# Latent attention heads: row maxima, scores and splits in another order and on another engine

## The chip, the cores and the metric

The kernel runs on one core of a Trainium2 chip. The metric is the device time of one launch in microseconds. Engines: TensorE (PE; its weight loads are shown apart, as PEld), VectorE (DVE), ScalarE (ACT), GpSimd (POOL), and SyncE (SP), whose queue issues most DMAs.

## The reference

Two transformer layers on 1024 positions of width 1024, float32. The change touches the mixer of the first, latent attention with 12 causal heads of width 96 (64 without and 32 with rotary position):

```
q = (rmsnorm(c_q) @ w_uq).reshape(b, s, 12, 96)        # rope on the last 32
k = concat([k_nope, rope(k_r) for every head])
sc = einsum('bqhd,bkhd->bhqk', q, k) * 96 ** -0.5
p = softmax(where(k_idx <= t_idx, sc, -1e30))
o = einsum('bhqk,bkhd->bqhd', p, v)                    # v: 64 wide
```

Memory cross-attention, an output projection, a second mixer and two large MLPs follow; they take most of the time and are untouched.

## The kernel before

**Precision.** A float32 operand x is split in two (helper `split`, L96): hi is a copy made by ScalarE (L99) in the type that TensorE reads fast, lo = x - hi, the rest, by VectorE (L100). A product is then three: hi hi, hi lo, lo hi.

**Head operands.** `head_tiles(h)` (L868) loads a head's queries and keys by four DMAs into q32 and k32 (96x1024, one buffer each; in the trace q and k) and splits them into qh, ql, kh, kl. Three sets of these are used in turn; the set of heads 1, 4, 7, 10 lies in older tiles and is called ckh and ckl in the trace. It is called two heads ahead, at the first block of head h - 2.

**Row maxima.** Softmax needs each query row's maximum before the scores. `row_max(h, i)` (L897) makes row tile i (128 queries): a product of the high parts over (i+1)*128 keys into a tile psx (L908), and a VectorE instruction that adds the causal mask `wide` and reduces to a column m (L915). For i > 3 psx is one tile of two banks with one buffer; lower rows use the common one-bank tiles, of which there are six. `max_row(h)` (L886) transposes the eight columns (psxt, L889), copies them (mh, L894) and writes them by a DMA (L895) into row 96 of qh, so that the score product subtracts the maximum by itself.

**Blocks.** A head has 12 score blocks (G, k): keys of tile k against query half G. Blocks with k >= 4G lie on the diagonal; their first 128 columns are masked, and at diagonal offset c = k - 4G they are 512 - 128c wide. Their order is the list `blocks` (L1006). `scores` (L1032) makes three products into a tile pss (L1023), and a fourth for the mask where `mask_by_pe` says so; else VectorE adds it (L1045). ScalarE takes the exponential into p (L1047, 12 buffers). GpSimd adds the p of a head up in acc (L1060).

**Order.** All products of this loop go on TensorE in the order in which the code issues them (L1178 ff.): block n of all heads; then the row maxima that the table `WHEN` sets there, as pairs (row, distance in blocks from the start of the head before; row 8 is `max_row`); every six blocks `values` (p times v, tile pso); after block 7 the `sums` of the head before (acc times ones, psd). `evac` and the stores of the denominators go through SP's queue. Heads 0 to 5, 6 to 9 and 10 are divided by their sums in later blocks (`rc_split`, `rc_mul`: loads of tiles rb, multiplies on VectorE). From block 116 on, weights of the output projection are split too (woq).

Of the kernel before, what the change touches and what calls it, by code (L numbers as in the profile page):

```python
# [55 lines left out]
def trunk(  # L56
# [25 lines left out]
    def ps1(name):  # L82
        return psum[0].tile([P, 512], F32, tag="m", bufs=4 if len(psum) == 1 else 6, name=name)
# [12 lines left out]
    def split(src, hi, lo, scale=None):  # L96

        if scale is None:
            a = nc.scalar.activation(hi, src, AF.Copy)  # L99
            d = nc.vector.tensor_tensor(lo, src, f32(hi), ALU.subtract)  # L100
        else:
            a = nc.scalar.activation(hi, src, AF.Copy, scale=scale)
            d = nc.vector.scalar_tensor_tensor(lo, src, scale, f32(hi), ALU.mult, ALU.subtract)
        return a.ins, d.ins
# [765 lines left out]
    def head_tiles(h):  # L870
        r = slice((h % 2) * 64, (h % 2) * 64 + 64)
        q32 = hb.tile([96, S], F32, tag="q32", bufs=1, name=f"q32_{h}")
        k32 = hb.tile([96, S], F32, tag="k32", bufs=1, name=f"k32_{h}")
        nc.sync.dma_start(out=q32[0:64], in_=qn[h // 2][r, :])
        nc.sync.dma_start(out=q32[64:96], in_=qr[h // 4][(h % 4) * 32 : (h % 4) * 32 + 32, :])
        nc.sync.dma_start(out=k32[0:64], in_=kn[h // 2][r, :])
        nc.sync.dma_start(out=k32[64:96], in_=krs)
        qh, ql, kh, kl = bufs_[h % 3]
        if h in (1, 2):
            head_ones(h)  # L880
        split(q32, qh[0:96], ql[0:96])
        split(k32, kh[0:96], kl[0:96])

    m8s, wide = {}, []

# [12 lines left out]
    def row_max(h, i):  # L898
        if h not in m8s:
            m8s[h] = hb.tile([P, NT], F32, tag="m8", bufs=2, name=f"m8_{h}")  # L900
        qh, ql, kh, kl = bufs_[h % 3]
        n = (i + 1) * P
        ps = psx(f"psx{h}_{i}") if i > 3 else ps1(f"psx{h}_{i}")
        cuts = [(0, 320), (320, 640)] if n == 640 else [(a, min(a + 512, n)) for a in range(0, n, 512)]
        if n == 640:
            ps = ps[:, 192:]
        for a, b in cuts:
            mm = nc.tensor.matmul(ps[:, a:b], qh[0:96, i * P : (i + 1) * P], kh[0:96, a:b], start=True, stop=True, skip_group_check=True)  # L908
        m = m8s[h][:, i : i + 1]
        least = 3.0e38  # L910
        if h == 0 and i:
            nc.vector.reduce_max(m, ps[:, : n - P], axis=AX, negate=True)
            least = m
        o, k = (ps[:, n - P : n], dmask) if h == 0 else (ps[:, :n], wide[0][:, S - n :])
        nc.vector.tensor_tensor_reduce(o, o, k, -1.0, least, ALU.add, ALU.min, accum_out=m)  # L915
        return mm.ins
# [86 lines left out]
    nc.gpsimd.tensor_copy(identr, ident)  # L1003
    nc.gpsimd.tensor_copy(maskr, dmaskT)

    blocks = [(1, 0), (0, 0), (1, 4), (0, 1), (1, 5), (1, 1), (0, 2), (1, 6), (1, 2), (0, 3), (1, 7), (1, 3)]  # L1006
    blocks_end = [(1, k) for k in (0, 4, 5, 6, 7, 1, 2, 3)] + [(0, k) for k in range(4)]

    def mask_by_pe(h, G, k):
        return k >= 4 * G and (k % 2 == 1 or h in (0, 1, 7, 9, 10, 11))  # L1010


    def blocks_of(h):
# [15 lines left out]

        return [(part ^ G, max(c0, part * 256), part * 256 + 256) for part in range(2) if c0 < part * 256 + 256]  # L1030

    def scores(h, G, k):  # L1032

        qh, ql, kh, kl = bufs_[h % 3]
        c0 = col0(G, k)
        ks = slice(k * P, (k + 1) * P)
        qs = slice(G * 512 + c0, G * 512 + 512)
        ps = ps1(f"pss{h}_{G}_{k}")[:, c0:]
        product(ps, kh[:, ks], qh[:, qs], start=True, stop=False)
        product(ps, kh[:, ks], ql[:, qs], start=False, stop=False)  # L1040
        if mask_by_pe(h, G, k):
            product(ps[:, 0:P], identr, maskr, start=False, stop=False)
        product(ps, kl[:, ks], qh[:, qs], start=False, stop=True)
        if k >= 4 * G and not mask_by_pe(h, G, k):
            nc.vector.tensor_tensor(ps[:, 0:P], ps[:, 0:P], dmaskT, ALU.add)  # L1045
        p = at.tile([P, 512], F32, tag="p", bufs=12, name=f"p{h}_{G}_{k}")
        masked[0:1] = [nc.scalar.activation(p[:, c0:], ps, AF.Exp, scale=SC).ins]  # L1047
        probs[(h, G, k)] = p
        if (h, "acc") not in acc_:
            acc_[(h, "acc")] = at.tile([P, 1024], F32, tag="acc", bufs=2, name=f"acc{h}")  # L1050
        a = acc_[(h, "acc")][:, G * 512 : G * 512 + 512]
        if (h, G) not in first_p:
            first_p[(h, G)] = p
            return
        q = first_p[(h, G)]
        if q is not None:
            first_p[(h, G)] = None
            if c0:
                nc.scalar.activation(a[:, :c0], q[:, :c0], AF.Copy)
        nc.gpsimd.tensor_tensor(a[:, c0:], p[:, c0:], (a if q is None else q)[:, c0:], ALU.add)  # L1060
# [85 lines left out]
    def rc_mul(c):  # L1146
# [17 lines left out]
    seq = [(h,) + b for h in range(H) for b in blocks_of(h)]  # L1164

    WHEN = {
# [3 lines left out]
    }  # L1170
    ahead = {}
    for h in range(1, H):
        for i, d in WHEN[min(h, 3)]:
            ahead.setdefault((h - 1) * NB + d, []).append((h, i))
    muls = iter(())
    cuts = [*range(0, (H - 1) * NB, 6), *range((H - 1) * NB, len(seq) + 1, 4)]
    batches = {b + 1: (a, b) for a, b in zip(cuts, cuts[1:])}
    for n in range(len(seq) + 2):  # L1178
        if n < len(seq):
            scores(*seq[n])  # L1180
        for g, i in ahead.get(n, ()):
            with queued():
                last_mm[0:1] = [row_max(g, i) if i < NT else max_row(g)[-1]]
        if n in batches:
            values(seq[slice(*batches[n])])
            h, j = divmod(n, NB)
            if j == 1 and h < H:
                evac(h - 1)
            if h and j == (7 if h < H - 1 else 5):
                sums(h - 1)  # L1190
            if n == len(seq) - 3:
                sums(H - 1, 1)
                last_o(1, at.tile([P, 256], F32, tag="on", bufs=2, name="rq1"))
        h, j = divmod(n, NB)
        if n < len(seq):
            if h and j == 0 and h + 2 < H:
                head_tiles(h + 2)
            if n == 5:
                with tc.issue_after(masked[0]):
                    head_tiles(2)  # L1200
        if n % 2 or n > 11 * NB:
            next(muls, None)
        if n >= 9 * NB + 8 and n % 3 == 0:
            wq.step()
        for c in range(3):
            if n == GRP[c + 1] * NB + (8 if c == 2 else 10):
                rc_split(c)
            if n == GRP[c + 1] * NB + (9 if c == 2 else 13):
                muls = rc_mul(c)
# [1115 lines left out]
```

## Time and profile before

| | us |
|---|---|
| median of 3 runs | 2089.3 (2088.59 to 2093.86) |
| profiled execution | 2089.84 |
| its span | 2088.1 |
| TensorE busy in it | 2060.1 |
| VectorE busy in it | 1433.5 |
| ScalarE busy in it | 1090.2 |
| GpSimd busy in it | 258.3 |

The span is the time from the first to the last instruction; 1.7 us of the execution lie outside it. All times of single instructions are counted from the span's start. The heads of the latent attention run from about 239 to 432 us. In a row of the order of time, a bracket at the end is the idle time of that engine just before, and what ended it; `x3` means three instructions shown together.

### The profile page before, as it was taken

What the parts mean: (1) busy time and instruction counts of PE and PEld (TensorE: products, weight loads), DVE (VectorE), ACT (ScalarE), POOL (GpSimd) and SP (SyncE); (2) the same over time, 40 slices, a digit from 0 to 9 for tenths busy, and PEclk for the clock granted to TensorE, in tenths of its full rate; (3) what the DMA queues carried; (4) which work ended last, traced back from release to release, by engine and by line L of the source; (5) the groups of instructions that cost most, each with busy time, mean ns of one, the idle gap of its engine ahead of it and who ended that gap; (6) DMA issues with size and microseconds to landing.
All of it is one profiled execution on the core that took longest, in us unless ns stands there. A gap on an engine that the chain in (4) does not pass through costs nothing.

```text
span 2088.1 us, 29578 instructions
## 1 busy us (share of the span) xinstructions
PE 2060.1 (99%) x10067; PEld 1684.8 (81%) x10067; DVE 1433.5 (69%) x2829; ACT 1090.2 (52%) x2359; POOL 258.3 (12%) x363
## 2 busy tenths in 40 slices
PE   9999999999999999999999999999999999999998
PEld 6988777678888888888888888778888888888887
DVE  8766566665977777976557535666977776976565
ACT  7554355566745544444445435766755544444453
POOL 1001256621000000000011133420000000000000
PEclk9999899999999999999999999999999999999999
DMA  6302223352444546944443544542344546945442
GB/s 225 104 1 77 57 69 76 112 162 86 147 153 141 166 161 234 331 124 153 142 118 104 147 106 125 139 135 78 136 150 158 166 146 227 331 139 156 121 121 87
DMA packets 183496, 292.88 MB, mean 140 GB/s; under 512 B 17707, under 2 KB 73456, under 8 KB 183344
## 3 DMA queue, kind: packets, MB, share of 16 engines
q1 hardware_dynamic: 177680, 275.17, 42.2%
q0 software_dynamic: 4144, 13.14, 1.7%
q10 hardware_dynamic: 1520, 2.68, 0.4%
q8 instruction: 79, 1.29, 0.3%
q14 instruction: 73, 0.60, 0.1%
HBM read 187.60 MB, written 81.44 MB: 129 GB/s over the span
## 4 chain that ended last, share of the span: by engine, by line
PE 94%; DVE 2%; ACT 1%; DMA 1%; issue 1%; SPq 0%; ACTq 0%; DVEq 0%
PE psy L1899 6%; PE psy L1897 6%; PE psy L1898 6%; PE psu L1560 6%; PE psu L1561 5%; PE psu L1559 5%; PE psz L1899 4%; PE psz L1897 4%; PE psz L1898 4%; PE psv L1560 4%; PE psv L1561 4%; PE psv L1559 4%; PE pss L1023 4%; PE pswo L111 3%; PE pswo L109 3%; PE pswo L110 3%
## 5 line engine op out<-in xcount | busy, mean ns | idle before, releaser
L99 ACT ACTIVATE g<-i 128x512 fp32r<-128x512 f32 x79 | 49.9, 631 | 104.1 <-PE psy L1898 53.3
L1897 PE MATMUL psy<-g 128*128 128x512 f32 x256 | 100.0, 391 | 0.0
L1898 PE MATMUL psy<-g 128*128 128x512 f32 x256 | 99.7, 389 | 0.0
L1899 PE MATMUL psy<-g 128*128 128x512 f32 x256 | 99.7, 389 | 0.0
L1060 POOL TENSOR_TENSOR acc<-p,acc 128x384 f32<-128x384 f32 (+3 forms) x96 | 93.7, 994 | 31.9 <-ACT p L1047 30.5
L915 DVE CUSTOM_DVE_ANT_0 psx<-psx,wide 128x1024 f32<-128x1024 f32 (+5 forms) x88 | 66.4, 765 | 43.8 <-PE psx L908 42.8
L100 DVE TENSOR_TENSOR g<-i,g 128x512 fp32r<-128x512 f32 x79 | 55.7, 705 | 51.7 <-ACT g L99 51.7
L1047 ACT ACTIVATE p<-pss 128x512 f32<-128x512 f32 (+3 forms) x144 | 67.2, 487 | 41.8 <-PE pss L1023 30.6
L99 ACT ACTIVATE uh<-i 128x512 fp32r<-128x512 f32 x66 | 41.6, 631 | 85.2 <-PE psz L1898 39.2
L99 ACT ACTIVATE i<-mr 128x512 fp32r<-128x512 f32 x78 | 47.9, 630 | 72.7 <-PE psy L1898 23.7
L100 DVE TENSOR_TENSOR uh<-i,uh 128x512 fp32r<-128x512 f32 x66 | 45.6, 691 | 46.5 <-ACT uh L99 46.5
L1899 PE MATMUL psz<-g 128*128 128x512 f32 x192 | 74.7, 389 | 0.0
L1897 PE MATMUL psz<-g 128*128 128x512 f32 x192 | 74.7, 389 | 0.0
L1898 PE MATMUL psz<-g 128*128 128x512 f32 x192 | 74.7, 389 | 0.0
L1458 ACT ACTIVATE mr<-mr,gcol 128x256 f32<-128x256 f32 (+1 forms) x160 | 64.0, 477 | 11.6 <-DMA mr<-in_mlp_w_up_dram 11.6
L100 DVE TENSOR_TENSOR i<-mr,i 128x512 fp32r<-128x512 f32 x78 | 53.7, 688 | 21.6 <-ACT i L99 21.6
L2017 POOL TENSOR_TENSOR wsr<-wsr,gcol 128x1024 f32<-128x1024 f32 x12 | 23.0, 1918 | 345.8 <-ACT i L99 276.7
L1779 DVE TENSOR_TENSOR mqq<-mqf,mqq 128x512 f32<-128x512 f32 x64 | 43.2, 688 | 22.7 <-DMA mqf<-in_mlp_w_down_dram 22.6
L1899 PEld LDWEIGHTS psy<-g 128*128 128x128 f32 x256 | 48.1, 188 | 10.0
L1897 PEld LDWEIGHTS psy<-g 128*128 128x128 f32 x256 | 48.1, 188 | 9.8
L1898 PEld LDWEIGHTS psy<-g 128*128 128x128 f32 x256 | 48.1, 188 | 9.8
L1023 PE MATMUL pso<-p,v 128*64 128x256 f32 (+1 forms) x480 | 54.6, 371 | 0.0
(670 smaller groups left out, 6825.6 us busy)
## 6 DMA issues: line engine op xcount, KB each, us to landing
i<-hd SPq DMA_DIRECT2D x154, 256.0 KB
hd<-uh SPq DMA_DIRECT2D x76, 256.0 KB
hd<-ul SPq DMA_DIRECT2D x76, 256.0 KB
mr<-in_mlp_w_up_dram SPq DMA_DIRECT2D x36, 512.0 KB
hd<-x SPq DMA_DIRECT2D x72, 256.0 KB
mr<-hd SPq DMA_DIRECT2D x70, 256.0 KB
d<-in_mlp_w_up_dram SPq DMA_DIRECT2D x32, 512.0 KB
mqf<-in_mlp_w_down_dram SPq DMA_DIRECT2D x32, 512.0 KB
```

What stands on the lines that cost most here:

```text
L99: a = nc.scalar.activation(hi, src, AF.Copy)
L100: d = nc.vector.tensor_tensor(lo, src, f32(hi), ALU.subtract)
L915: nc.vector.tensor_tensor_reduce(o, o, k, -1.0, least, ALU.add, ALU.min, accum_out=m)
L1023: last_mm[0:1] = [nc.tensor.matmul(*args, skip_group_check=True, **kw).ins]
L1047: masked[0:1] = [nc.scalar.activation(p[:, c0:], ps, AF.Exp, scale=SC).ins]
L1060: nc.gpsimd.tensor_tensor(a[:, c0:], p[:, c0:], (a if q is None else q)[:, c0:], ALU.add)
L1559: nc.tensor.matmul(ps, wh[:, k, :], xh[:, k, :], start=p in (1, 2, 5) and k == 0, stop=False, skip_group_check=True)
L1560: nc.tensor.matmul(ps, wh[:, k, :], xl[:, k, :], start=False, stop=False, skip_group_check=True)
L1561: nc.tensor.matmul(ps, wl[:, k, :], xh[:, k, :], start=False, stop=k == 3, skip_group_check=True)
L1897: nc.tensor.matmul(ps, ah[:, j, :], bh, start=start, stop=False, skip_group_check=True)
L1898: nc.tensor.matmul(ps, ah[:, j, :], bl, start=False, stop=False, skip_group_check=True)
L1899: nc.tensor.matmul(ps, al[:, j, :], bh, start=False, stop=k == NP - 1, skip_group_check=True)
```

## The change

1. `head_tiles`: for heads 2 to 11 the rests ql and kl are made by GpSimd instead of VectorE. The high parts stay on ScalarE.
2. Blocks (0,3) and (1,2) change places in `blocks`.
3. `mask_by_pe`: TensorE masks the diagonal offsets 0 and 1, before 1 and 3, in heads 2 to 6 and 8. Heads 0, 1, 7, 9, 10, 11 still mask all on TensorE.
4. `scores` takes one or two blocks. A block of offset 3 (128 columns) waits for the next one if that is not on the diagonal. For two blocks the first two products of each are issued, the wide block first, then the last product of each.
5. `WHEN`: the rows of all heads come earlier and in other distances.
6. `row_max` of head 0 takes its two-bank tile for all rows.

```
-        split(q32, qh[0:96], ql[0:96])
-        split(k32, kh[0:96], kl[0:96])
+        for src, hi, lo in ((q32, qh, ql), (k32, kh, kl)):
+            if h < 2:
+                split(src, hi[0:96], lo[0:96])
+            else:
+                nc.scalar.activation(hi[0:96], src, AF.Copy)
+                nc.gpsimd.tensor_tensor(lo[0:96], src, f32(hi[0:96]), ALU.subtract)
...
-        ps = psx(f"psx{h}_{i}") if i > 3 else ps1(f"psx{h}_{i}")
+        ps = psx(f"psx{h}_{i}") if i > 3 or len(psum) == 1 else ps1(f"psx{h}_{i}")
...
-    blocks = [(1, 0), (0, 0), (1, 4), (0, 1), (1, 5), (1, 1), (0, 2), (1, 6), (1, 2), (0, 3), (1, 7), (1, 3)]
+    blocks = [(1, 0), (0, 0), (1, 4), (0, 1), (1, 5), (1, 1), (0, 2), (1, 6), (0, 3), (1, 2), (1, 7), (1, 3)]
...
-        return k >= 4 * G and (k % 2 == 1 or h in (0, 1, 7, 9, 10, 11))
+        return k >= 4 * G and (k % 4 < 2 or h in (0, 1, 7, 9, 10, 11))
...
-    def scores(h, G, k):
-
-        qh, ql, kh, kl = bufs_[h % 3]
+    def scores(*todo):
+
+        tiles = []
+        for h, G, k in todo:
+            qh, ql, kh, kl = bufs_[h % 3]
+            c0 = col0(G, k)
+            ks = slice(k * P, (k + 1) * P)
+            qs = slice(G * 512 + c0, G * 512 + 512)
+            ps = ps1(f"pss{h}_{G}_{k}")[:, c0:]
+            product(ps, kh[:, ks], qh[:, qs], start=True, stop=False)
+            product(ps, kh[:, ks], ql[:, qs], start=False, stop=False)
+            tiles.append((ps, kl[:, ks], qh[:, qs]))
+        for (h, G, k), (ps, kl_, qh_) in zip(todo, tiles):
+            if mask_by_pe(h, G, k):
+                product(ps[:, 0:P], identr, maskr, start=False, stop=False)
+            product(ps, kl_, qh_, start=False, stop=True)
+        for block, tile in zip(todo, tiles):
+            probabilities(*block, tile[0])
...
-        3: ((7, -5), (6, -4), (5, -2), (4, 0), (3, 1), (2, 2), (1, 3), (0, 4), (8, 6)),
+        3: ((7, -7), (6, -5), (5, -4), (4, -2), (3, 0), (2, 1), (1, 2), (0, 3), (8, 5)),
...
     for n in range(len(seq) + 2):
         if n < len(seq):
-            scores(*seq[n])
+            waiting.append(seq[n])
+            if n == len(seq) - 1 or seq[n][2] - 4 * seq[n][1] < 3 or seq[n + 1][2] - 4 * seq[n + 1][1] >= 0:
+                scores(*waiting[::-1])
+                waiting.clear()
```

`probabilities` is the rest of the old `scores`: VectorE's mask, the exponential, GpSimd's add. The rows of WHEN for sets 1 and 2 become `((7, 0), (3, 0), (6, 2), (2, 2), (5, 4), (1, 4), (4, 5), (0, 6), (8, 8))` and `((7, -4), (6, -3), (5, -2), (4, 0), (3, 1), (2, 2), (1, 3), (0, 4), (8, 6))`; before, they were `((7, 2), (3, 3), (6, 4), (2, 5), (5, 6), (1, 7), (4, 8), (0, 9), (8, 10))` and `((7, -2), (6, -1), (5, 0), (4, 1), (3, 2), (2, 3), (1, 4), (0, 5), (8, 6))`.

In the rows of the order below pss3_1_7 is the score tile of head 3, G = 1, k = 7, and psx5_6 is row 6 of head 5's maxima; qh0, kh2 and so on are the operands of a head; the number at the end of a name only counts tiles.

TensorE in head 3 before, from row 6 of the maxima of head 5 to row 5:

```order
L908 MATMUL psx5_6_3201<-kh2_2529,qh2_2527 128x512
L908 MATMUL psx5_6_3201<-kh2_2529,qh2_2527 128x384
L1023 MATMUL pss3_0_3_3205<-qh0_1949,kh0_1951 128x128
L1023 MATMUL pss3_0_3_3205<-ql0_1950,kh0_1951 128x128
L1023 MATMUL pss3_0_3_3205<-maskr_2538,identr_2537 128x128
L1023 MATMUL pss3_0_3_3205<-qh0_1949,kl0_1952 128x128
L1023 MATMUL pss3_1_7_3213<-qh0_1949,kh0_1951 128x128
L1023 MATMUL pss3_1_7_3213<-ql0_1950,kh0_1951 128x128
L1023 MATMUL pss3_1_7_3213<-maskr_2538,identr_2537 128x128
L1023 MATMUL pss3_1_7_3213<-qh0_1949,kl0_1952 128x128
L908 MATMUL psx5_5_3221<-kh2_2529,qh2_2527 128x512
L908 MATMUL psx5_5_3221<-kh2_2529,qh2_2527 128x256
```

After, TensorE in the same head from row 7 to row 6:

```order
L912 MATMUL psx5_7_3150<-kh2_2529,qh2_2527 128x512 x2
L1027 MATMUL pss3_0_2_3154<-qh0_1949,kh0_1951 128x256
L1027 MATMUL pss3_0_2_3154<-ql0_1950,kh0_1951 128x256
L1027 MATMUL pss3_0_2_3154<-qh0_1949,kl0_1952 128x256
L1027 MATMUL pss3_1_6_3162<-qh0_1949,kh0_1951 128x256
L1027 MATMUL pss3_1_6_3162<-ql0_1950,kh0_1951 128x256
L1027 MATMUL pss3_1_6_3162<-qh0_1949,kl0_1952 128x256
L912 MATMUL psx5_6_3170<-kh2_2529,qh2_2527 128x512
L912 MATMUL psx5_6_3170<-kh2_2529,qh2_2527 128x384
```

Then values and sums, and after them, still on TensorE, from row 5 to row 4 with the first pair between them:

```order
L912 MATMUL psx5_5_3198<-kh2_2529,qh2_2527 128x512
L912 MATMUL psx5_5_3198<-kh2_2529,qh2_2527 128x256
L1027 MATMUL pss3_1_2_3202<-qh0_1949,kh0_1951 128x512
L1027 MATMUL pss3_1_2_3202<-ql0_1950,kh0_1951 128x512
L1027 MATMUL pss3_0_3_3205<-qh0_1949,kh0_1951 128x128
L1027 MATMUL pss3_0_3_3205<-ql0_1950,kh0_1951 128x128
L1027 MATMUL pss3_1_2_3202<-qh0_1949,kl0_1952 128x512
L1027 MATMUL pss3_0_3_3205<-qh0_1949,kl0_1952 128x128
L912 MATMUL psx5_4_3217<-kh2_2529,qh2_2527 128x320 x2
```

The narrow blocks and their masks no longer stand between rows 6 and 5; rows 7 and 6 have two blocks of 256 columns between them, rows 5 and 4 one pair.

TensorE at the turn from head 0 to head 1 before, rows 7, 6 and 5 of set 2:

```order
L908 MATMUL psx2_7_2697<-kh2_2529,qh2_2527 128x512 x2
L1023 MATMUL pss0_1_3_2701<-qh0_1949,kh0_1951 128x512
L1023 MATMUL pss0_1_3_2701<-ql0_1950,kh0_1951 128x512
L1023 MATMUL pss0_1_3_2701<-qh0_1949,kl0_1952 128x512
L908 MATMUL psx2_6_2708<-kh2_2529,qh2_2527 128x512
L908 MATMUL psx2_6_2708<-kh2_2529,qh2_2527 128x384
L1023 MATMUL pss1_1_0_2712<-ckh_554,ckl_555 128x512 x3
L908 MATMUL psx2_5_2719<-kh2_2529,qh2_2527 128x512
```

and after:

```order
L912 MATMUL psx2_7_2674<-kh2_2529,qh2_2527 128x512 x2
L1027 MATMUL pss0_1_2_2678<-qh0_1949,kh0_1951 128x512
L1027 MATMUL pss0_1_2_2678<-ql0_1950,kh0_1951 128x512
L1027 MATMUL pss0_0_3_2681<-qh0_1949,kh0_1951 128x128
L1027 MATMUL pss0_0_3_2681<-ql0_1950,kh0_1951 128x128
L1027 MATMUL pss0_1_2_2678<-qh0_1949,kl0_1952 128x512
L1027 MATMUL pss0_0_3_2681<-maskr_2538,identr_2537 128x128
L1027 MATMUL pss0_0_3_2681<-qh0_1949,kl0_1952 128x128
L912 MATMUL psx2_6_2693<-kh2_2529,qh2_2527 128x512
L912 MATMUL psx2_6_2693<-kh2_2529,qh2_2527 128x384
L912 MATMUL psx2_5_2697<-kh2_2529,qh2_2527 128x512
L912 MATMUL psx2_5_2697<-kh2_2529,qh2_2527 128x256
```

Row 5 now follows row 6 directly.

GpSimd at the end of head 3 before, the last adds of that head and the first of the next:

```order
L1060 TENSOR_TENSOR acc3_3066<-p3_1_2_3198,acc3_3066 128x512
L1060 TENSOR_TENSOR acc3_3066<-p3_0_3_3210,acc3_3066 128x128
L1060 TENSOR_TENSOR acc3_3066<-p3_1_7_3218,acc3_3066 128x128
L1060 TENSOR_TENSOR acc3_3066<-p3_1_3_3229,acc3_3066 128x512
L1060 TENSOR_TENSOR acc4_3238<-p4_1_4_3280,p4_1_0_3236 128x512
```

and after:

```order
L1074 TENSOR_TENSOR acc3_3070<-p3_1_2_3210,acc3_3070 128x512
L1074 TENSOR_TENSOR acc3_3070<-p3_0_3_3214,acc3_3070 128x128
L886 TENSOR_TENSOR kl0_1952<-k32_6_3247,kh0_1951 96x1024
L1074 TENSOR_TENSOR acc3_3070<-p3_1_3_3229,acc3_3070 128x512
L1074 TENSOR_TENSOR acc3_3070<-p3_1_7_3233,acc3_3070 128x128
L886 TENSOR_TENSOR ql0_1950<-q32_6_3246,qh0_1949 96x1024
L1074 TENSOR_TENSOR acc4_3242<-p4_1_4_3283,p4_1_0_3240 128x512
```

The two rests of head 6 stand among the last adds of head 3.

## Rows read from the trace of the kernel before

**Rows 1.** The page's first part: engine, busy us, share of span, instructions.

```profile
PE 2060.1 (99%) x10067; PEld 1684.8 (81%) x10067; DVE 1433.5 (69%) x2829; ACT 1090.2 (52%) x2359; POOL 258.3 (12%) x363
```

**Rows 2.** Busy time by stretch: columns as the first row says; head 1's start, heads 3 and 8.

```profile
core 0: us, PE busy (x) PEld busy (x) DVE busy (x) ACT busy (x) POOL busy (x), PEclk, DMA share, GB/s
256.00:263.00 7.00, 6.91 (x26) 4.60 (x27) 4.01 (x7) 1.98 (x4) 0.00 (x0) 0.51 0.45 97
287.00:302.00 15.00, 14.60 (x102) 10.79 (x101) 9.83 (x22) 8.66 (x18) 9.58 (x10) 1.00 0.32 72
365.00:381.00 16.00, 13.68 (x91) 9.76 (x92) 13.90 (x26) 7.99 (x16) 11.56 (x10) 1.00 0.42 115
```

**Rows 3.** TensorE's waits, 240 to 432: us in total, times, longest.

```profile
PE psx L908 <- DVE m L915: 5.6, 11, 1.1
PE psxt L889 <- DVE m L915: 1.4, 2, 1.2
```

**Rows 4.** Order of time, head 3: start, us, instruction; from psx6 to psx5.

```profile
302.19 0.57 PE L908 MATMUL psx<-kh,qh 96*128 96x512 f32 x2
...
302.66 0.28 PE L1023 MATMUL pss<-ql,kh 97*128 97x128 f32 x1
...
302.80 1.10 DVE L915 CUSTOM_DVE_ANT_0 psx<-psx,wide 128x896 f32<-128x896 f32 x1 [3.10 <-PE psx L908]
...
303.81 0.14 DVE L915 DVE_READ_ACCUMULATOR2_ANT m<- 128x1 f32 x1
...
304.01 0.62 PE L908 MATMUL psx<-kh,qh 96*128 96x512 f32 x2 [0.41 <-DVE m L915]
```

**Rows 5.** Order of time, head 3: row 7's product and its result.

```profile
297.73 0.63 PE L908 MATMUL psx<-kh,qh 96*128 96x512 f32 x2
...
299.55 0.14 DVE L915 DVE_READ_ACCUMULATOR2_ANT m<- 128x1 f32 x1
```

**Rows 6.** Order of time, head 2: row 5's product and its result.

```profile
288.75 0.62 PE L908 MATMUL psx<-ckl,ckh 96*128 96x512 f32 x2 [0.41 <-DVE m L915]
...
290.29 0.14 DVE L915 DVE_READ_ACCUMULATOR2_ANT m<- 128x1 f32 x1
```

**Rows 7.** Order of time, TensorE: score products of 512, 256 and 128 columns.

```profile
254.68 0.86 PE L1023 MATMUL pss<-ckh,ckl 97*128 97x512 f32 x3
...
289.21 0.40 PE L1023 MATMUL pss<-qh,kh 97*128 97x512 f32 x1
...
296.92 0.28 PE L1023 MATMUL pss<-qh,kh 97*128 97x256 f32 x1
...
297.03 0.27 PE L1023 MATMUL pss<-ql,kh 97*128 97x256 f32 x1
...
318.15 0.50 PE L1023 MATMUL pss<-ckh,ckl 97*128 97x128 f32 x3
```

**Rows 8.** Order of time, TensorE, head 3: six blocks' values.

```profile
298.30 2.60 PE L1023 MATMUL pso<-p,v 128*64 128x256 f32 x24
```

**Rows 9.** Order of time, TensorE, in head 1: row 5 of set 2.

```profile
256.09 0.96 PE L908 MATMUL psx<-kh,qh 96*128 96x512 f32 x2 [0.55 <-DVE m L915]
```

**Rows 10.** Order of time, head 8: k's load, its copy, and who waits.

```profile
371.34 0.59 SPq L877 DMA_DIRECT2D k<-krs  x1
...
375.44 1.06 ACT L99 ACTIVATE ckl<-k 96x1024 fp32r<-96x1024 f32 x1 [0.70 <-ACT mh L894]
...
376.55 0.73 PE L908 MATMUL psx<-ckl,ckh 96*128 96x512 f32 x2 [1.95 <-ACT ckl L99]
```

**Rows 11.** Groups by form: line, operation, count, busy us, mean ns, idle before.

```profile
L1060 POOL TENSOR_TENSOR acc<-p,acc 128x512 f32<-128x512 f32 x36 | 49.7, 1382 | 29.1 <-ACT p L1047 28.0
...
L2017 POOL TENSOR_TENSOR wsr<-wsr,gcol 128x1024 f32<-128x1024 f32 x12 | 23.0, 1918 | 345.8 <-ACT i L99 276.7
...
L1060 POOL TENSOR_TENSOR acc<-p,acc 128x128 f32<-128x128 f32 x24 | 11.0, 477 | 0.2
...
L100 DVE TENSOR_TENSOR ql<-q,qh 96x1024 fp32r<-96x1024 f32 x7 | 9.8, 1396 | 0.0
```

**Rows 12.** Order of time, GpSimd, head 8: four adds.

```profile
374.74 6.02 POOL L1060 TENSOR_TENSOR acc<-p,acc 128x384 f32<-128x384 f32 x4
```

More of the change, by code (lines that the diff above doesn't have):

```diff
@@ L1030, in quarters, with probabilities @@
         return [(part ^ G, max(c0, part * 256), part * 256 + 256) for part in range(2) if c0 < part * 256 + 256]
-    def scores(h, G, k):
-        qh, ql, kh, kl = bufs_[h % 3]
-        c0 = col0(G, k)
[L1036 to L1043, printed above, removed]
+    def scores(*todo):
[15 more added lines that the diff above has]
+            probabilities(*block, tile[0])
+    def probabilities(h, G, k, ps):
+        c0 = col0(G, k)
         if k >= 4 * G and not mask_by_pe(h, G, k):
@@ L1175, in trunk @@
     muls = iter(())
+    waiting = []
     cuts = [*range(0, (H - 1) * NB, 6), *range((H - 1) * NB, len(seq) + 1, 4)]
```

4 rows, old and new, of the table WHEN are left out of this document.

## Prediction

> **What bounds the kernel now.** I read the busy times of the engines first: TensorE computes in 99% of the span [rows 1]. So a change saves time only where it takes TensorE work away, or one of TensorE's few waits. The whole change lies in the latent-attention heads, about 239 to 432 us of the span. There I read busy times by head, to see who has room: in a plain head of 15 us TensorE is busy 14.60, VectorE 9.83, ScalarE 8.66, GpSimd 9.58 [rows 2]. No helper is near its limit; a faster VectorE is worth nothing by its busy time alone. Then TensorE's waits in that stage: 5.6 us in 11 waits for row maxima on VectorE and 1.4 in two waits of the transpose psxt [rows 3], and one of 1.95 in head 8 [rows 10]. About 9 us in all is what can be won here; what can be lost has no such limit.
>
> Last I read how a row-max wait comes about, in the order of time [rows 4]. The psx tile has one buffer. psx6 (row 6) starts on TensorE at 302.19, VectorE's reduction starts at 302.80 and its result is read out by 303.81 + 0.14; the next row, psx5, starts at 304.01, so 0.06 after that, and 1.82 after psx6 started. For row 7 the same sum gives 299.55 + 0.14 + 0.06 - 297.73 = 2.02 [rows 5], for row 5 290.29 + 0.20 - 288.75 = 1.74 [rows 6]; that row 5 had itself waited, which I take to delay it by one weight load, 0.11 (below), so 1.63 without. **The rule:** between the starts of two row-max products must lie 2.02, 1.82 or 1.63 us of TensorE work, plus 0.11 for the weights of a product that has waited; what is missing is lost.
>
> What lies between them is priced by rows too [rows 7]: score products of 512 columns follow each other every (0.86 - 0.40)/2 = 0.23 us, of 256 columns every 297.03 - 296.92 = 0.11, of 128 columns every (0.50 - 0.28)/2 = 0.11, where the single one of 0.28 stands in [rows 4]. The narrow ones are no cheaper than those of 256; I read that as a floor set by their weight loads. The row-max products of rows 7, 6 and 5 (1024, 896 and 768 columns) are 0.47, 0.41 and 0.35 at 0.23 per 512.
>
> **The change part by part.**
>
> 1. *Subtractions of heads 2 to 11 from VectorE to GpSimd: 20 instructions.* They take 1.4 us each on VectorE [rows 11], some 28 us that VectorE gets back. That lies beside TensorE's work, and VectorE began a reduction right after TensorE's product as it was [rows 4], so I price the gain at 0. On GpSimd no subtraction of 96x1024 stands in the trace. Bounds: 1.92, from a 128x1024 multiply, and 2.59, from the adds drawn on (477 ns at 128 columns, 1382 at 512, so 302 per 128 more) [rows 11]. I take 2.5, since the adds run in the same stretch beside the same engines. A head's period is 304.01 - 288.75 = 15.26 (psx5 of two heads in a row, [rows 4, 6]); a plain head then has 9.6 + 2 x 2.5 = 14.6 of it on GpSimd, by the bounds 13.4 to 14.8. It fits, with little room. The adds queue behind a subtraction and the sums wait for the adds; the sums of a head come only after block 7 of the next, about half a head after its last adds, which is more than one subtraction. Cost 0 while that cover holds; the rival below prices the other case. In front of each subtraction GpSimd waits for ScalarE's copy; behind it in GpSimd's row stand the adds of the last two blocks. Loads into q32 and k32 (one buffer each) now wait for GpSimd, and with them SP's queue: the stores of the denominators and of the outputs behind them are needed a head later.
> The Trainium skill ("GPSIMD Engine Reference", section "4.1 Engine selection") speaks against this part: an elementwise operation with two inputs belongs on VectorE, GpSimd being about twice as slow. Its 4497 ns for 2048 columns would make an estimate of 2.25 here, between the bounds above, and the sum would not move.
>
> 2. *Pairs.* Block (0,3) or (1,7), 128 columns wide, is scored with the 512-wide block behind it. Same products, same widths; at the spacings above the sum is unchanged: 0. Could narrow products behind wide ones be cheaper (their weights loaded in the shadow of 0.23 us of streaming)? They go at the price of 128 columns, (0.23/4 = 0.06) instead of 0.11, at best: two such per pair, 23 pairs, 0.05 each, 2.3 us to win. No row shows it; below as a rival, 0 in the sum.
>
> 3. *Masks.* Of the 72 mask products none goes and none comes: 0 on TensorE. The VectorE masks move from offsets 0 and 2 to 2 and 3 in seven heads: 0.
>
> 4. *Row maxima earlier (the table WHEN).* This is where the sum is made.
> - Before, sets 3 to 11: psx6 and psx5 have eight narrow products between them: 0.41 + 8 x 0.11 = 1.31 of 1.93 needed, 0.62 lost. That is the 0.41 of [rows 4] plus the late weights. The other neighbours have values and sums between them (2.60 us of values alone, [rows 8]) or wide blocks.
> - After, in heads whose offsets 2 and 3 are masked on VectorE: psx7 and psx6 have six products of 256 between them: 0.47 + 6 x 0.11 = 1.16 of 2.13 needed: 0.97 lost. psx6 to psx5 is covered by values and sums. psx5 and psx4 have one pair between them: 0.35 + 3 x 0.23 + 3 x 0.11 = 1.38 of 1.74 needed: 0.36 lost. Together 1.33, so 0.71 more than before. In heads 1, 7 and 9 three mask products more lie between them: about 1.0, 0.38 more. Sets 3 to 11 are made in heads 1 to 9: 6 x 0.71 + 3 x 0.38 = **+5.4**.
> - Start (sets 1 and 2 in heads 0 and 1). Before: one wait for psxt1 and two of 0.69 and 0.55, the last at 256.09 [rows 9]; with late weights and refilling 2.4 by the rule. After, by the rule: 0.63 (psx1_6), 0.58 (psx1_4), 0.51 (psx2_6) and 1.52 (psx2_5, which follows psx2_6 with nothing between): 3.2. **+0.8**. Behind the waits of before the clock falls: granted 0.51 over the 7 us from 256 [rows 2], that is 1.2 instead of 2.4 GHz; at 0.49 x 7 it costs 3.4 us. After, the waits come at about the same place and are longer, so I leave those 3.4 as they are.
>
> 5. *Loads of heads 8 to 10.* In head 8 the first row-max product waits 1.95 for ScalarE's ckl, which waits for the load of k issued at 371.34 [rows 10]. After, that load stands ahead of the reciprocal tiles' loads in SP's queue: **-1.9**. The tiles' loads then come behind, and with them some multiplies of VectorE ahead of reductions in set 9: **+0.4**, taken between 0 and 1.4 (one multiply the size of a subtraction [rows 11]). The two waits of psxt and the last set's, where VectorE splits weights, stay: 0, give or take 1.5.
>
> **Sum:** 5.4 + 0.8 - 1.9 + 0.4 = +4.7 on the 2089.84 of the profiled execution (span 2088.1 and 1.7 around it), so 2094.5. That execution is 0.5 above the median of 2089.3: **2094.0**. A measurement of this kernel tells about 0.3% from no change, that is 2083.0 to 2095.6.
>
> **The rivals.**
> - *The clock does not fall in the start.* Other places and lengths of waits may leave it whole. For: the rows from 263 on are at full clock, and the 1.95 of head 8 was followed by no fall [rows 2]. Against: more is waited in the start than before. 2094.0 - 3.4 = 2090.6.
> - *Slower: steady waits drop the clock.* Each head now loses 0.97 and 0.36 within some 6 us; before, one loss of 0.62 left the clock at 1.00 [rows 2]. If a head's waits set it off as those of the start did, each time costs 3.4 [rows 2]: in three heads of nine +10, in five +17: 2104 to 2111. It decides from about one head on (over 2095.6).
> - *Slower: GpSimd becomes the bound.* From (15.3 - 9.6)/2, some 2.9 us a subtraction in plain heads. For: four adds took 6.02 in head 8 [rows 12], and GpSimd 11.56 us there instead of 9.58 [rows 2]. If that were the rule, 2 x 2.5 + 11.56 - 15.3 = 1.3 over per head, nine heads: +11, 2105. Against: those adds ran beside VectorE's subtractions, which are what goes away. The Trainium skill ("SBUF — State Buffer", section "Who interferes with whom") says that a VectorE instruction with two SBUF inputs contends with a GpSimd instruction that reads SBUF; by that the move takes this very contention away.
> - *Faster: the free VectorE takes the waits away.* If the reductions were late because of subtractions queued ahead of them, -(5.6 + 1.4 + 1.9) and no clock fall, -3.4: 2089.3 - 12.3 = 2077. Against: 302.80 is 0.2 after the end of psx6's product; the reduction itself is the wait [rows 4].
> - *Pairs make narrow products cheaper*: -2.3 against the sum, 2092; with the wait behind psx5 longer by what the pair is shorter, somewhat more is left.
> The Trainium skill ("TensorE: Matmul & The Clock Gate", section "Back-to-back issue gap") has weight loads pulled ahead through a reorder window, 81 ns sustained at 128 columns; the trace has 0.11. By 81 ns this rival would be half of its price.
>
> **How the numbers follow.** Forecast (losses by the rule, clock falls once as before) 0.45: 2091 to 2097.5, by set 9, set 11 and the spacings; two thirds of it within the bound, one third above. Clock whole 0.18, within. Clock falls in steady heads 0.15, slower. GpSimd bound 0.07, slower. VectorE's freedom 0.10, faster. Pairs cheaper 0.05, within. Faster 0.10; same 0.30 + 0.18 + 0.05 = 0.53; slower 0.15 + 0.15 + 0.07 = 0.37. The range goes from 2086.5 to 2104: it leaves out the faster case and about half of the two slower ones, 0.2 in all. The side stays nearly open: more than half of the chance is no measurable change.
>
> **What would show it.** Right: in every plain head a wait of psx6 of about 0.8 shown (0.97 less late weights) and one of psx4 of about 0.2, none of psx5; the ckl wait of 1.95 gone; GpSimd busy some 14.5 us per head, its subtraction between 1.9 and 2.6; half a clock once, near 256. Wrong: granted clock under 1 in heads 2 to 9; waits of the sums for GpSimd's adds, or of ql and kl products for its subtractions; row-max waits that shrink, which would say that VectorE's queue and not its reduction set them; narrow products spaced 0.06 in the pairs.

## The result and the profile after

The changed kernel takes 2096.9 us in the median, the kernel before 2090.1 in the same comparison: a ratio of 1.0025 with an interval of 1.0015 to 1.0035, so 3 to 7 us slower. The forecast was 2094.0, range 2086.5 to 2104. Executions of one kernel lie several us apart here (the changed one 2094.0 to 2098.5, at a mean granted clock of 0.996 to 0.993); the profiled ones, 2098.15 after and 2089.84 before, are 8.3 apart.

The page of the changed kernel answers [rows 1]: VectorE has 17 us less to do, GpSimd 40 more, TensorE 6 more.

```profile
PE 2066.5 (99%) x10067; PEld 1688.1 (81%) x10067; DVE 1416.1 (68%) x2809; ACT 1088.7 (52%) x2359; POOL 298.2 (14%) x383
```

TensorE's waits in the stage (236 to 445 us) answer [rows 3]: 9.1 us for row maxima instead of 5.6, and one wait of a transpose of 5.5. The wait for ckl of [rows 10] is gone from the list.

```profile
PE psx L912 <- DVE m L919: 9.1, 13, 2.1
PE psxt L893 <- DVE m L919: 5.5, 1, 5.5
```

Busy time by stretch, columns as in [rows 2]: a part of the changed kernel ahead of the heads, three places at which the granted clock is near half, and the window that [rows 2] has for head 3.

```profile
214.00:224.00 10.00, 10.00 (x47) 8.13 (x46) 7.03 (x19) 2.26 (x3) 0.00 (x0) 1.00 0.19 44
...
248.00:260.00 12.00, 10.95 (x39) 7.89 (x40) 3.67 (x8) 4.75 (x8) 8.80 (x8) 0.57 0.29 68
368.00:376.00 8.00, 8.00 (x32) 5.24 (x32) 4.08 (x9) 3.69 (x7) 4.05 (x3) 0.57 0.30 103
396.00:405.00 9.00, 5.05 (x20) 3.74 (x22) 7.79 (x11) 2.05 (x5) 5.65 (x6) 0.50 0.35 114
...
287.00:302.00 15.00, 14.20 (x98) 10.31 (x98) 6.92 (x20) 8.45 (x18) 13.33 (x12) 1.00 0.31 73
```

Where the 8.3 us went is read best from marks that both traces have on TensorE: the first score product, and the sums (psd) of each head, which stand after block 7 of the next.

| mark on TensorE | before | after | growth since the last mark | forecast for it |
|---|---|---|---|---|
| first score product | 239.52 | 233.77 | -5.75 | none |
| sums of head 0 | 270.30 | 267.59 | +3.04 | +0.8 |
| sums of head 5 | 346.59 | 346.54 | +2.66 | about +3.5 |
| sums of head 6 | 362.19 | 362.32 | +0.18 | about +0.5 |
| sums of head 7 | 379.74 | 383.78 | +3.91 | about -1 |
| sums of head 8 | 396.66 | 407.39 | +6.69 | about +0.5 |
| sums of head 9 | 412.49 | 421.68 | -1.54 | 0 |
| end of the span | 2088.1 | 2096.4 | -0.89 | 0 |

So the closeness of the time hides three things that the forecast did not have: a gain ahead of the heads, and two losses late in the stage.

**Ahead of the heads.** In the kernel before, the first row maximum of head 0 waits for qh, and the clock falls behind it. First the row of before from the order of time, then its stretch (in the changed kernel this stretch is the one at 1.00 above), last the same product in the changed kernel, with no wait:

```profile
215.77 0.80 PE L908 MATMUL psx<-kh,qh 96*128 96x128 f32 x2 [3.14 <-ACT qh L99]
```

```profile
214.00:224.00 10.00, 8.23 (x25) 6.77 (x26) 4.13 (x13) 1.32 (x2) 0.00 (x0) 0.66 0.16 39
```

```profile
217.19 0.40 PE L912 MATMUL psx<-kh,qh 96*128 96x128 f32 x2
```

**Plain heads.** Order of time of the changed kernel, TensorE in heads 3 and 4: a pair, then rows 7 and 6 of a set, which answer [rows 4] and [rows 7].

```profile
302.15 0.40 PE L1027 MATMUL pss<-ql,kh 97*128 97x512 f32 x1
302.39 0.23 PE L1027 MATMUL pss<-qh,kh 97*128 97x128 f32 x1
302.45 0.27 PE L1027 MATMUL pss<-ql,kh 97*128 97x128 f32 x1
302.56 0.51 PE L1027 MATMUL pss<-qh,kl 97*128 97x512 f32 x2
...
309.78 0.70 PE L912 MATMUL psx<-kh,qh 96*128 96x512 f32 x2
...
311.86 0.67 PE L912 MATMUL psx<-kh,qh 96*128 96x512 f32 x2 [0.67 <-DVE m L919]
```

Row 6 starts 2.08 after row 7 and has waited 0.67, where 2.13 and about 0.8 were forecast. In the pair the narrow product behind a wide one takes 302.45 - 302.39 = 0.06, the next one 0.11.

**Head 7.** Order of time of the changed kernel: GpSimd ends a subtraction at 355.33 + 2.39; only then can SP issue the next load into the same buffer, and behind it in SP's queue stand the loads of rb. VectorE's multiplies by the reciprocals (L1169) wait for those; row 5 of set 9 is reduced behind them; row 4 waits on TensorE for that, and then comes the stretch from 368 above.

```profile
355.33 2.39 POOL L886 TENSOR_TENSOR ql<-q,qh 96x1024 fp32r<-96x1024 f32 x1
...
357.75 0.52 SPq L874 DMA_DIRECT2D q<-fa  x1
...
359.85 2.46 SPq L1149 DMA_DIRECT2D rb<-rcd  x4
...
363.57 0.69 DVE L1169 TENSOR_TENSOR qn<-rb,qn 128x512 f32<-128x512 f32 x1 [2.51 <-DMA rb<-rcd]
...
365.04 0.69 DVE L1169 TENSOR_TENSOR qn<-rb,qn 128x512 f32<-128x512 f32 x1 [0.78 <-DMA rb<-rcd]
...
365.65 0.96 DVE L919 CUSTOM_DVE_ANT_0 psx<-psx,wide 128x768 f32<-128x768 f32 x1
...
366.72 0.56 PE L912 MATMUL psx<-kh,qh 96*128 96x320 f32 x2 [2.12 <-DVE m L919]
```

**Heads 8 and 9.** VectorE's split of a weight takes 6.42 us; GpSimd works without a gap in that time. The last reductions of set 10 stand behind the split, and the transpose waits 5.48.

```profile
392.56 2.39 POOL L886 TENSOR_TENSOR ql<-q,qh 96x1024 fp32r<-96x1024 f32 x1
394.92 2.20 POOL L1074 TENSOR_TENSOR acc<-p,p 128x512 f32<-128x512 f32 x2
397.09 3.19 POOL L1074 TENSOR_TENSOR acc<-p,acc 128x384 f32<-128x384 f32 x2
...
392.74 6.42 DVE L100 TENSOR_TENSOR woq<-wor,woq 128x1024 fp32r<-128x1024 f32 x1 [2.50 <-ACT woq L99]
...
399.95 0.37 PE L893 MATMUL psxt<-ident,m 128*8 128x128 f32 x1 [5.48 <-DVE m L919]
```

### The profile page after: what moved, and what is told of

The parts are those of the page before. It is cut to its first block, busy times and chain, and to the rows that moved or that the text cites. A ratio compares the mean times of both kernels' runs of the same rounds, so it can differ in the third digit from the quotient of the medians.

```text
span 2096.4 us, 29613 instructions
## 1 busy us (share of the span) xinstructions
PE 2066.5 (99%) x10067; PEld 1688.1 (81%) x10067; DVE 1416.1 (68%) x2809; ACT 1088.7 (52%) x2359; POOL 298.2 (14%) x383
## 4 chain that ended last, share of the span: by engine, by line
PE 92%; issue 2%; DVE 2%; DMA 1%; ACT 1%; POOL 0%; SPq 0%; DVEq 0%; POOLq 0%; ACTq 0%
PE psy L1916 6%; PE psy L1917 6%; PE psy L1915 5%; PE psu L1579 5%; PE psu L1577 5%; PE psu L1578 5%; PE psz L1916 4%; PE psz L1917 4%; PE psz L1915 4%; PE psv L1579 4%; PE psv L1577 4%; PE psv L1578 4%; PE pss L1027 3%; PE pswo L111 3%; PE pswo L109 3%; PE pswo L110 3%
## 5 line engine op out<-in xcount | busy, mean ns | idle before, releaser
L1074 POOL TENSOR_TENSOR acc<-p,acc 128x512 f32<-128x512 f32 (+2 forms) x96 | 86.7, 917 | 33.8 <-ACT p L1061 31.5
```

## The experiments

Ratios are against the kernel before, run on the same chip, with 95% intervals. First each part alone, on the kernel before.

**e1_two_bank** (only edit 6) and **e2_rests** (only edit 1, with the lines of the change):

```
e1:  -        ps = psx(f"psx{h}_{i}") if i > 3 else ps1(f"psx{h}_{i}")
     +        ps = psx(f"psx{h}_{i}") if i > 3 or len(psum) == 1 else ps1(f"psx{h}_{i}")
```

> The kernel before with edit 6 alone: all row maxima of head 0 in the two-bank tile. In the trace of before TensorE waits 3.14 us for qh of head 0 and its clock falls behind that wait; in the trace after neither is there, and the first score product comes 5.75 us earlier. Theory: this edit alone does it, by moving the row-max products of head 0 some 25 products later: about 5.5 us faster, 2084.5. Rival: that wait belongs to the single execution or to another edit: no change, 2090.

2083.8 us, ratio 0.9964 (0.9951 to 0.9978). Its first score product stands at 233.77, to the hundredth where the changed kernel has it. The row maxima of head 0 stand outside the loop that is ordered by hand, and nothing but their tile was changed: they now come behind other products, and qh is there. Edit 6 alone is a gain.

> The kernel before with edit 1 alone: rests of heads 2 to 11 on GpSimd. Theory: GpSimd's unbroken run of adds and subtractions holds up a VectorE subtraction with both operands in SBUF, here the splits of the output projection's weights near 390 to 399 us; that costs a wait of TensorE and a fall of the clock, less the 1.95 of head 8 that the other order of loads saves: 2 to 8 us slower, 2092 to 2098. Rival, as predicted: GpSimd's work is hidden, 0 to 2 us faster, 2088 to 2090.

2092.1, ratio 1.0005 (0.9996 to 1.0014): by the ratio some 1 us slower, between the two. In its trace the wait for ckl is gone; instead there are a wait of 1.18 for row 4 of set 9 and one of 2.27 for set 10's transpose, with a granted clock of 0.66 and 0.64 in the 9 us behind each. Where GpSimd's last subtraction and VectorE's second split of a weight overlap, both take longer:

```profile
388.27 3.43 POOL L886 TENSOR_TENSOR ql<-q,qh 96x1024 fp32r<-96x1024 f32 x1
...
390.24 2.55 DVE L100 TENSOR_TENSOR woq<-wor,woq 128x1024 fp32r<-128x1024 f32 x1
```

**e3_when** (only the new table WHEN) and **e4_pairs** (only block order, masks, pairs):

> The kernel before with edit 5 alone: the new table of row maxima. The prediction's sum for this part is +0.8 in the start and about +5.4 in the plain heads, less what the narrow blocks between rows differ without pairs: 2095 to 2097. If the multiplies that wait for their loads stand in front of a row maximum in head 8 without the GpSimd move as well, and the clock falls there, up to 5.5 more: 2101. Rival: the table costs only together with GpSimd's subtractions: 2090.

2094.5, ratio 1.0013 (1.0004 to 1.0022): 3 us over the kernel before in the same comparison, about half of the 5 to 7 expected. A plain head takes 15.88 instead of 15.26, 0.62 more, with waits of 0.67 and 0.27 shown at rows 6 and 4. The rule has 0.97 lost at row 6 and, with eight narrow products and no pair in front of row 4, 1.74 - 0.35 - 8 x 0.11 = 0.51 there; less the 0.62 of before that is 0.86 more, so it is too high here.

> The kernel before with edits 2 to 4 alone: block order, masks, pairs; row maxima, rests and head 0 as before. Predicted for TensorE: 0; with the table of before, row 6 to row 5 now has one pair between them, 0.41 + 1.03 = 1.44 of 1.93, 0.49 lost instead of 0.62, so about 1 us faster in all: 2089. Rival, narrow products cheaper in pairs: 2.3 us faster still, 2086.5.

2081.8, ratio 0.9951 (0.9938 to 0.9963): far better than both theories. A plain head takes 14.98, and from the sums of head 6 to those of head 8 it takes 30.8 us instead of 34.5: the wait for ckl and that of the transpose have gone. Why the first goes, SP's queue shows: the second load of k (L877) for head 10 now stands ahead of the loads of rb. First e4; then the kernel before, which has it at 371.34 [rows 10], behind them:

```profile
350.71 0.57 SPq L877 DMA_DIRECT2D k<-krs  x1
...
353.23 2.47 SPq L1145 DMA_DIRECT2D rb<-rcd  x4
```

```profile
357.03 2.47 SPq L1135 DMA_DIRECT2D rb<-rcd  x4
```

Why that of the transpose goes is not settled. Together the four parts alone give some -14 us; made together they give +7.

**e5_head11, e6_late_mul, e7_both, e9_after_dve** take the suspects out of the changed kernel:

```
e5:  -            if h < 2:
     +            if h < 2 or h == 11:
e6:       rbs = [rc_pair(c, j, i) for j, i in todo[:2]]
          yield
     +    yield
     +    yield
e9:  -            if h < 2:
     +            if h >= 0:
```

> The changed kernel with the rests of head 11 alone back on VectorE. In its trace one VectorE split of weights takes 6.42 us instead of 1.2 to 1.6, beside GpSimd's subtraction of head 11 and the adds right in front of and behind it; the transpose of head 10 waits 5.48 for it, and the clock falls behind that. Theory: GpSimd's stream holds VectorE up; without head 11's two subtractions there the split takes under 2.6 and 5 to 9 us come back: 2088 to 2092. Rival: adds alone hold it up as long, or it has another cause: no change, 2097.

2094.5, ratio 1.0021 (1.0012 to 1.0030). The mechanism is right: the splits take 1.2 to 1.5 and the wait of 5.48 is gone. The time is not: now rows 6 and 4 of set 11 wait 1.14 and 1.88 behind other splits, and the clock is at 0.57 from 404 to 412.

> The changed kernel with the multiplies by the reciprocals started four blocks later behind their first loads. In the trace of the changed kernel row 5 of set 9 is reduced behind a multiply that waits for its load, row 4's product on TensorE waits 2.12 for that, and the clock falls behind it. Theory: the multiplies in front are what delays it: the wait goes, and with the clock 3 to 5.5 us: 2091.5 to 2094. Rival: the multiplies then stand in front of other reductions of the next rows and cost the same there: 2097.

2094.5, ratio 1.0033 (1.0019 to 1.0046): the rival. Row 5's reduction stands behind a multiply still, and the wait is 3.46 instead of 2.12.

> The changed kernel with both: head 11's rests on VectorE and the multiplies four blocks later. Theory: two separate stalls, so the gains add: 8 to 14 us, 2083 to 2089. Rival: one stall taken away is paid at the other place: about the better of the two alone, 2090.

2095.5, ratio 1.0029 (1.0019 to 1.0040): no gain, so nearer the rival, though its 2090 is missed too. Row 4 of set 9 still waits 2.09, and rows 6 and 4 of set 11 wait 1.14 and 1.70.

> The changed kernel with all rests on VectorE (edit 1 undone). Edits 1, 6, 5 and 2 to 4 alone gave about +1, -7.7, +3 and -10 us against the kernel before, -14 in sum, where all together gave +5 to +7. Theory: what is missing, some 19 us, comes from edit 1 meeting the others; without it head 10's stall is gone, and what stays are the losses of the table in the plain heads: 2080 to 2088. Rival: the table and the pairs lose it between them, with or without edit 1: 2093 to 2097.

2093.5, ratio 1.0015 (1.0004 to 1.0026): again the rival. With everything on VectorE there is a wait of 2.95 in head 8, where row 7 of set 10 is reduced behind a subtraction of 1.75 us and a multiply of 1.48, and plain heads take 15.77 as in the changed kernel. From the sums of head 6 to those of head 7 it takes 20.07 us, against 21.46 in the changed kernel (the profiled execution, at 2088.3, lies 5 us below the median). So edit 1 alone is not what eats the 19 us. As long as the rows come early, something stands in front of some reduction. The next three take the table back.

**e10_old_when, e11_best, e12_spaced**: the changed kernel with the old WHEN; that with all rests on VectorE too; and that with a table spaced by the rule:

```
e12: 2: ((7, -3), (6, -1), (5, 1), (4, 2), (3, 3), (2, 4), (1, 5), (0, 6), (8, 8)),
     3: ((7, -5), (6, -4), (5, -1), (4, 1), (3, 2), (2, 3), (1, 4), (0, 5), (8, 7)),
```

> The changed kernel with the table of row maxima of before (edit 5 undone; rests on GpSimd, head 0, blocks, masks and pairs stay). Theory now: the earlier row maxima lose it, since every reduction that stands in VectorE's queue behind a multiply, a weight split or another wait now has TensorE waiting for it, and each such wait of 2 us or more is followed by the half clock; edit 1 costs little. So this is as fast as edits 6 and 2 to 4 together, less about 1: 2073 to 2079. Rival: GpSimd's subtractions keep their stall in head 10 (5.5 and the clock): 2081 to 2085.

2088.1, ratio 0.9992 (0.9983 to 1.0001): no difference from before, against both, and slower than the rival.

> The kernel before with edits 6 and 2 to 4 (no rests on GpSimd, table of before). Alone they gave 7.7 and 9.7. If they add: 2072 to 2074. Rival: head 0's shift moves the loads of the next heads, and part of the other gain with it: 2076 to 2080.

2077.0, ratio 0.9931 (0.9918 to 0.9944): most of both gains add, but the time is that of the rival.

These two differ by edit 1 alone, and by 11 us. In plain heads they are equal (sums of head 0 to head 6: 90.34 and 90.36 us). The loss is in two places: sums of head 6 to head 7, 22.65 against 15.20, and head 8 to head 9, 19.18 against 15.64. The first, in the order of time of e10, is the chain of head 7 above: GpSimd ends head 9's subtraction; only then can SP issue the load of head 10's queries into the same buffer; behind it in SP's queue stand the loads of rb; VectorE's multiply waits for them, row 6 of set 9 is reduced behind it, and row 5 on TensorE waits 3.60.

```profile
347.63 2.39 POOL L886 TENSOR_TENSOR ql<-q,qh 96x1024 fp32r<-96x1024 f32 x1
...
350.05 0.52 SPq L874 DMA_DIRECT2D q<-fa  x1
...
352.36 2.46 SPq L1149 DMA_DIRECT2D rb<-rcd  x4
...
356.13 0.69 DVE L1169 TENSOR_TENSOR qn<-rb,qn 128x512 f32<-128x512 f32 x1 [3.44 <-DMA rb<-rcd]
...
359.75 1.01 PE L912 MATMUL psx<-kh,qh 96*128 96x512 f32 x2 [3.60 <-DVE m L919]
```

The clock behind that wait, in the stretches of e10:

```profile
356.00:368.00 12.00, 8.40 (x29) 6.18 (x30) 6.82 (x13) 3.97 (x8) 6.18 (x5) 0.60 0.28 94
```

In e11 VectorE ends that subtraction 2 us earlier, and the load of head 10's queries stands behind the loads of rb instead of in front of them; those go out 3.2 us sooner:

```profile
346.85 1.21 DVE L100 TENSOR_TENSOR ql<-q,qh 96x1024 fp32r<-96x1024 f32 x1
...
349.18 2.48 SPq L1149 DMA_DIRECT2D rb<-rcd  x4
...
351.77 0.54 SPq L874 DMA_DIRECT2D q<-fa  x1
```

Edit 1 is the only difference between the two kernels, so it brings both the later end of the subtraction and the other order of SP's queue; which of them weighs more is not shown. In the second place, beside and behind head 11's subtractions, two splits of weights take 2.32 and 1.66 us on VectorE (1.23 and 1.53 in e11); row 5 of set 11 waits 1.34 for the reduction behind the second, and the clock is at 0.60 in the 8.6 us after that; in e11 it waits 0.82, and the clock stays at 1.00.

> As e11_best, with a table of row maxima that spaces rows 6, 5 and 4 of the plain heads so far apart that by the rule of the prediction none waits, and set 2 likewise but for one wait of about 0.5. By the rule, against e11_best: 0.49 in nine heads less, and 1 us in the start: 4 to 5 us faster, 2068 to 2070; 3.4 more if the clock then stays up in the start. Rival: later rows run into the next head's work and wait there: no gain.

2073.9, ratio 0.9915 (0.9900 to 0.9929), the fastest; 3 us under e11 and less than the rule gave. In the profiled execution, which at 2077.6 lies 3.7 above the median, two transposes now wait 1.98 and 1.33. In plain heads the rule holds: 14.50 us from sums to sums against 14.99 in e11, 0.49 less, and no wait shown. First e12, then e11:

```profile
289.04 0.64 PE L1027 MATMUL psd_None<-acc,ones 128*32 128x256 f32 x8
...
303.54 0.64 PE L1027 MATMUL psd_None<-acc,ones 128*32 128x256 f32 x8
```

```profile
279.26 0.64 PE L1027 MATMUL psd_None<-acc,ones 128*32 128x256 f32 x8
...
294.25 0.64 PE L1027 MATMUL psd_None<-acc,ones 128*32 128x256 f32 x8
```

**e13_two_heads**: e10 with two of the ten heads back on VectorE (`if h < 2 or h in (9, 11)`).

> e10_old_when with the rests of heads 9 and 11 alone back on VectorE. In e10_old_when the load of head 10's queries waits in SP's queue until GpSimd has done head 9's subtraction; the loads of the reciprocal tiles stand behind it, some 3 us later than in e11_best, VectorE's multiply waits for them with row 6 of set 9 behind it, TensorE waits 3.60, and the clock falls: 7.5 us in that head. In head 10 weight splits beside head 11's subtractions take 2.3 instead of 1.2 to 1.5, and 3.5 us go there. Theory: these two chains are all that edit 1 costs; with heads 9 and 11 on VectorE the wait of 3.60 goes under 0.5, head 10 comes within 1 us of e11_best, and the time within 2 us of it: 2076 to 2079. Rival: GpSimd's other subtractions do the same elsewhere (head 10's in head 8): 2083 to 2088.

2077.4, ratio 0.9932 (0.9919 to 0.9946): 11 us back, level with e11. (What the expectation calls head 10 is the stretch from the sums of head 8 to those of head 9.) The rb loads go out at 348.48, the load of head 10's queries behind them as in e11, row 5 waits 0.16, and the two stretches take 15.13 and 15.54 us instead of 22.65 and 19.18. The stretch between them takes 16.36 instead of 15.24 in e11, with a wait of 1.03. So the other eight heads' subtractions on GpSimd cost some 1 us there, and these two nearly all that edit 1 costs.

```profile
348.48 2.47 SPq L1149 DMA_DIRECT2D rb<-rcd  x4
...
351.04 0.54 SPq L874 DMA_DIRECT2D q<-fa  x1
...
356.26 0.62 PE L912 MATMUL psx<-kh,qh 96*128 96x512 f32 x2 [0.16 <-DVE m L919]
```

## Why the prediction was right, and where it was not

The time came 3 us from the forecast. Its largest term, the row maxima, was right in mechanism and too large; that the sum came so near is luck, since what it left out, -5.75 and about +11, has opposite signs.

**The rule for row maxima held.** Against e12, whose plain heads show no wait, the changed kernel's 15.77 (283.45 to 299.22) loses 1.27; the working had 1.33. The net was +0.51 a head and not +0.71 (and +0.18 instead of 0.38 in the one head with all masks on TensorE that can be read), so about +3.6 for the nine heads where the working has +5.4, for two small reasons: the loss went up by a bit less than 0.71, and the pairs give something. With the 0.62 that the working takes off, a head of before would be 14.64, so pairs and masks save about 0.14. The rival "pairs make narrow products cheaper" was thus true at part of its price: 0.06 behind a wide product, as it supposed, but only there, and the wide product behind a narrow one takes 0.28 instead of 0.23 (e12: starts at 291.12, 291.40 and 291.63), which gives most of it back. One reading in the working is off: in [rows 4] row 6's products end at 302.19 + 0.57 = 302.76, so VectorE's reduction begins 0.04 behind them and not 0.2, which only strengthens the argument that the reduction itself is the wait.

**Step 1, duration.** GpSimd's subtraction takes 2.38 us, 2.5 was taken; its busy time in head 3's window is 13.33 of 15. It did not become the bound of any plain head, and VectorE's freedom was worth little there (nothing in e10 against e11, 0.16 a head in e2): both as argued.

**Step 1, the queues, failed.** It says that with SP's queue held by GpSimd only stores wait that are "needed a head later". It left out the loads of rb in the same queue, whose reader, a multiply, stands in VectorE's queue ahead of a reduction that TensorE waits for. Step 5 has them, at +0.4; what they cost is 2.12 of waiting in the changed kernel and 3.60 in e10, and the clock each time. With the table of before, e10, e11 and e13 show the chain link by link; with the new table, taking it out (e9) leaves most of the loss, behind another wait. The wait of 1.9 is gone, but not by the step that the working gives: in the changed kernel k's second load still stands behind ten of the twelve loads of rb, at 370.50, ScalarE copies it at 377.42, later than before, and TensorE comes to it some 4 us late. In e2 and e4 the load does stand ahead of them, in e4 without any move of the rests.

**Step 1, contention, failed.** The working cited the Trainium skill ("SBUF — State Buffer", "Who interferes with whom") for the good side of the move: VectorE's subtractions of rests would no longer meet GpSimd's reads. The trace agrees with the rule (6.42 us beside GpSimd, 1.22 without), but four weight splits with two operands in SBUF stay on VectorE in heads 8 and 9, where GpSimd now has two more subtractions: 6.42 us for a split instead of 1.2 to 1.6, gone with head 11's subtractions on VectorE (1.23 to 1.47 in e5, 1.22 to 1.73 in e13). The place was in sight ("where VectorE splits weights, stay: 0, give or take 1.5"); the price was 5.48 and the clock.

**Edit 6 was not priced at all.** The working has no term for it, although the wait of 3.14 in front of head 0's row maxima stood in the trace of before, ahead of the stretch that was read. It is worth 5.75 in the profiles.

**The clock.** In the start it fell as forecast, for longer (0.57 over 12 us, [rows 2] has 0.51 over 7). In e6's execution, with the new table, and in e1's, with the old one, it did not fall there: from the first score product to the sums of head 0 they take 29.12 and 28.50 us, 0.62 apart where the working has +0.8. So the rest of +3.04 is the clock, which the working took to cost the same before and after. The rival of waits that drop the clock came true, but not by the plain heads' waits of 0.67, which left it at 1.00: it fell behind waits of 2.12 and 5.48.

**Parts that saturate.** The early table costs about 16 us without edit 1 (e9 against e11), edit 1 costs 11 with the old table (e10 against e11), and both together some 20 (the changed kernel against e11). In the profiles 4.4 of the table's 16 lie between the sums of head 0 and of head 6 (94.77 us in e9, 90.36 in e11). Taken back from the changed kernel, edit 1 gives 2 to 3 us (e9) and the table 7 to 9 (e10); e5 to e7 moved a wait and did not remove it. The forecast added the parts up, so its sum came out near for reasons that it did not have: -5.75 not seen, and about +11 not seen at the two places in heads 7 to 9, of which 1.5 comes back in the next head. What in e4 frees the transpose of its wait, and which part of the early table costs what in heads 7 to 9, stays open.

## What to carry to other kernels

When work goes to a slower helper, follow each buffer that it now frees later through the queue in which the next load waits, and what stands behind that load, up to an engine that the bound one waits for; look whether the order of that queue has changed too; and look for what stays on the old engine and meets the moved work. Price every line of a diff whose order shows instructions moved, also where no arithmetic changes. If a gain does not appear after one suspect is taken out, take out the other and then both: waits that sit in series hide each other.

## What the runs showed of the hardware

A VectorE subtraction of two SBUF operands was held to 6.42 us beside an unbroken row of GpSimd adds and subtractions, against 1.22 in the same trace with GpSimd idle (at 404.78); GpSimd's subtraction there took its usual 2.39. In e2 the same pair of neighbours shared the loss, 2.55 and 3.43 instead of 1.2 and 2.4. In e11 GpSimd bore it: its two adds took 3.83 instead of 2.20, and the split beside them 1.23.

```profile
379.74 3.83 POOL L1074 TENSOR_TENSOR acc<-p,p 128x512 f32<-128x512 f32 x2 [2.51 <-ACT p L1061]
...
381.48 1.23 DVE L100 TENSOR_TENSOR woq<-wor,woq 128x1024 fp32r<-128x1024 f32 x1 [0.38 <-ACT woq L99]
```

So either engine can be the one that waits; what decides it is not shown.

The granted clock stayed at 1.00 behind TensorE waits of 0.67 in every plain head. In the 8 us behind those of 2.12, 3.14, 3.60 and 5.48 it was 0.61, 0.62, 0.50 and 0.61. Between these it went both ways: behind one and the same wait of 1.95 it stayed at 1.00 in [rows 2] and fell in e1 (0.70 from 368 to 372), and behind the waits of the start, up to 1.25, it fell in the changed kernel and stayed at 1.00 in e6.
